# Attention's queries and keys with features on partitions, rotated there

## The chip, the cores and the metric

One core of a Trainium2 chip runs the whole program. The metric is the device time of one execution in microseconds, as the median of the timed runs. A profiled execution gives the trace from which the rows below are taken.

## What is computed

Two layers over 256 tokens of 1024 columns, in fp32: feed-forward, four mixers side by side, feed-forward. The mixers share one projection of the normed rows. The fourth is attention: 12 heads of 128 features (three groups of four, with different windows), whose queries and keys have their first 32 features rotated by an angle that grows with the position.

```python
def _partial_rope(x, positions):            # x: batch, tokens, heads, 128
    half = ROPE_DIM // 2                    # ROPE_DIM = 32
    inv_freq = ROPE_THETA ** (-jnp.arange(half) / half)
    ang = positions[..., None] * inv_freq
    cos, sin = jnp.cos(ang)[:, :, None, :], jnp.sin(ang)[:, :, None, :]
    x1, x2 = x[..., :half], x[..., half:ROPE_DIM]
    rot = jnp.concatenate([x1 * cos - x2 * sin, x2 * cos + x1 * sin], axis=-1)
    return jnp.concatenate([rot, x[..., ROPE_DIM:]], axis=-1)

def _dilated_attention(qkv, positions):
    ...
    q = _partial_rope(qkv[:, :, 0], positions)
    k = _partial_rope(qkv[:, :, 1], positions)
    v = qkv[:, :, 2]
    ...                                     # for each group: softmax(q k^T / sqrt(128), window) v
```

The other three mixers are a gated recurrence (HGRN2), a state-space model (S5) with a gated product "glu", and a convolution over 31 tokens. Each mixer's output passes a branch product, is gated and summed; then come an output product and the second feed-forward.

## The kernel before

Every product with weights is made of three matmuls in fp32r: weights and activations are each split exactly into a high and a low part, and high x high, high x low and low x high are summed in PSUM (`mm3`). `Stream` loads the weights in the order of their use (1 MB at a time on SP's queue, four buffers "raw"), and splits them slot by slot (128 x 1024): ScalarE writes the high part "whi", VectorE the low part "wlo" as a difference. Six and five buffers of these (`NW = 5`, line 29) let the splitting run ahead of TensorE.

There are two forms of product. `cols_tok` (line 803) has tokens on the output's partitions: the activations are stationary and 512 columns of weights move; two banks of 128 tokens, 24 matmuls each. It takes its slots one by one. `cols_feat` (line 849) has features on the output's partitions: weights are stationary, and all 256 tokens move; a bank holds two blocks of 128 features, 48 matmuls of 256 columns. It takes two slots at once.

Between the products run side jobs, generators for S5, the recurrence, the convolution and attention. A step of a job is issued at a `tick` inside a product, where the estimates kept by `Paced` say that its operands are there and that VectorE and ScalarE are not more than `LAG = 3.8` us (convolution: `LAST_LAG = 1.8`) behind TensorE (line 35). Each engine then works its instructions in that fixed order. Jobs have a priority: attention's rotation 0, attention 1, recurrence 2, convolution 3. `finish` issues what is left of a job where a product needs its result: S5 before "glu", the others before their branch (order of the branches: S5, recurrence, attention, convolution as number 2). Four PSUM banks "acc" take the products, four banks "mx" all side work.

`ORDER` (line 305) is the order of the mixers' products: i, u, f, q, g, then six attention chunks, the convolution's b and a, three more chunks, glu, gates and branches. An attention chunk is 512 columns by `cols_tok`: four pieces (a head's query, key or value of one group), in the order of `PIECES` (line 290): for each pair of heads all queries, then keys, then values. `ev_att` (line 1347) has ScalarE copy queries and keys from PSUM into "rq", values into "av". `rope_turn` (line 1323) rotates on VectorE ("ropeB", "ropeA", "rq": four instructions for both halves of the tokens, with tables "cosd" and "sind" by tokens), then TensorE turns each head's 128 x 128 onto feature partitions ("rt", banks of "mx"), and ScalarE copies the turned heads into "aq" and "ak". `attend` (line 1370) then multiplies queries and keys ("as"), masks, takes exponentials, turns the probabilities ("pTb") and multiplies with the values ("apv"). In the recurrence, "hd" and "hl" are small products; "y", "w", "yk" belong to S5.

Of the kernel before, what the change touches and what calls it, by code (L numbers as in the profile page):

```python
# [16 lines left out]
ALU = mybir.AluOpType  # L17
# [72 lines left out]
class ActCost:  # L90
    """With the loads of the functions' tables."""
# [22 lines left out]
class Stream:  # L114
    """Weights in the order of their use: loads, then an exact split into two 12-bit parts.

    A group is (loads, slots): loads are (source, blocks of 128 rows), slots (load, view -> part of it)."""

# [35 lines left out]
    def pump(self, n=1, ahead=True):  # L154
        """The low part of a slot whose high part is there, then the high part of the next."""
# [33 lines left out]
def trunk(ctx, tc, x_in, positions, ffn1_norm, ffn1_w_gate, ffn1_w_up, ffn1_w_down, mix_norm, w_in,  # L189
# [44 lines left out]
    def g_tok(w, pieces, n_loads=2):  # L234
        """512 columns in 2 or 4 loads; slots of 256 rows."""
# [11 lines left out]
    def g_feat(w, c0, n=512):  # L247
        """n columns; slots of 512 rows and 256 columns."""
# [8 lines left out]
    def g_rows_feat(w, order):  # L257
        """512 rows, 1024 columns; slots of all rows and 256 columns, given by the first columns of their halves."""
# [31 lines left out]
    PIECES = [(k, 2 * hp + e, g) for hp in range(2) for k in range(3) for g in range(3) for e in range(2)]  # L290

    def att_runs(i):
        return [(C_ATT + 1536 * k + 512 * g + P * h, 2 * P) for k, h, g in PIECES[4 * i:4 * i + 4:2]]

    def by_head(pieces):
        """Pairs of heads' pieces: (pair, which of it, head, kind, first group, number of pairs)."""
        a = 0
        while a < len(pieces):
            k, h, g = pieces[a]
            n = 2 if a + 2 < len(pieces) and pieces[a + 2][0] == k else 1  # L300
            for e in range(2):
                yield a // 2, e, h + e, k, g, n
            a += 2 * n

    ORDER = [("i",), ("u",), ("f",), ("q",), ("g",)] + [("att", i) for i in range(6)] + [("b",), ("a",)] + \
        [("att", i) for i in range(6, 9)] + \
# [57 lines left out]
    def grab(n=1):  # L364
        """Banks of the side work's own, held over several steps."""
# [50 lines left out]
    # rows of 128 features, turned into columns of scalars  # L416
# [28 lines left out]
    cosd = const([P, 2, 32], "cosd")  # L445
    sind = const([P, 2, 32], "sind")
# [15 lines left out]
    def masks():  # L462
        # the attention's masks: d = t - s
# [14 lines left out]
    def prepare():  # L478
        # the recurrence's masks: s in the left block whose right neighbour has t
# [10 lines left out]
        # columns  # L490
# [22 lines left out]
        # rotary tables  # L513
# [8 lines left out]
        # cos(a) = sin(pi/2 - |reduced a|)  # L522
# [4 lines left out]
        yield  # L527
        S.activation(sind[:, :, 16:32], red, AF.Sin)
# [19 lines left out]
        # S5: the discretized states of both layers, 128 states a column  # L548
# [24 lines left out]
        # mag - 1, by tanh where it is small  # L573
# [31 lines left out]
    # S5 of a layer: blocks of 4 tokens, t = 4 n + i; groups of 16 channels G = 16 jp + 2 jh + g,  # L605
    # states on partitions (g, p) and columns j = 8 jp + jh, a block's inputs on partitions (jp, i, c)
# [5 lines left out]
    def s5_tables(l):  # L612
# [15 lines left out]
        # powers of the states' factors  # L628
# [23 lines left out]
        # the discretized inputs' matrices  # L652
# [979 lines left out]
```

## Time and profile before

| | us |
|---|---|
| timed runs: median (lowest to highest of 3) | 1610.09 (1608.42 to 1613.12) |
| profiled execution, first to last instruction (span) | 1609.4 |
| TensorE busy (matmuls) | 1583.1 |
| VectorE busy | 1109.6 |
| ScalarE busy | 837.6 |
| GpSimd busy | 23.9 |

The busy time of an engine is a sum over the span; a matmul's recorded duration reaches beyond the start of the next one, because matmuls overlap, so that the distance between two starts is what a matmul takes of TensorE's time. Line 72 is the helper through which every instruction of the four engines is issued, so the rows are told apart by the names of the tiles. Layer 0's mixers run from some 210 to 617 us, layer 1's from some 1005 to 1411 us.

### The profile page before, as it was taken

What the parts mean: (1) busy time and instruction counts of PE and PEld (TensorE: products, weight loads), DVE (VectorE), ACT (ScalarE), POOL (GpSimd) and SP (SyncE); (2) the same over time, 40 slices, a digit from 0 to 9 for tenths busy, and PEclk for the clock granted to TensorE, in tenths of its full rate; (3) what the DMA queues carried; (4) which work ended last, traced back from release to release, by engine and by line L of the source; (5) the groups of instructions that cost most, each with busy time, mean ns of one, the idle gap of its engine ahead of it and who ended that gap; (6) DMA issues with size and microseconds to landing.
All of it is one profiled execution on the core that took longest, in us unless ns stands there. A gap on an engine that the chain in (4) does not pass through costs nothing.

```text
span 1609.4 us, 27748 instructions
## 1 busy us (share of the span) xinstructions
PE 1583.1 (98%) x11471; PEld 1442.8 (90%) x11471; DVE 1109.6 (69%) x1806; ACT 837.6 (52%) x1195; POOL 23.9 (1%) x53
## 2 busy tenths in 40 slices
PE   7999999999999999999999999999999999999998
PEld 6999788789899997999889988987899999989986
DVE  6778865876778866555478774567867898665553
ACT  5445455557565465444345544646565555654442
POOL 1000000000000000000000000000000000000000
PEclk9999999999999999999999999999999999999999
DMA  8565556444444456555555545664444545645551
GB/s 278 185 177 210 171 186 191 154 141 148 147 168 158 159 186 219 184 175 207 181 173 187 184 161 193 206 194 119 170 131 148 190 161 168 212 158 184 185 212 61
DMA packets 179519, 282.48 MB, mean 176 GB/s; under 512 B 26718, under 2 KB 82080, under 8 KB 179392
## 3 DMA queue, kind: packets, MB, share of 16 engines
q1 hardware_dynamic: 154240, 270.55, 49.7%
q10 hardware_dynamic: 24832, 9.97, 2.7%
q8 instruction: 90, 1.47, 0.4%
q14 instruction: 37, 0.30, 0.1%
q0 software_dynamic: 320, 0.18, 0.0%
HBM read 277.53 MB, written 3.15 MB: 174 GB/s over the span
## 4 chain that ended last, share of the span: by engine, by line
PE 94%; ACT 2%; DVE 2%; ACTq 1%; issue 1%; DMA 0%; SPq 0%; POOLq 0%; POOL 0%; DVEq 0%
PE down L72 15%; PE att_t L72 12%; PE up_h L72 12%; PE gate_h L72 12%; PE pgt_h L72 11%; PE br L72 6%; PE gate_t L72 3%; PE po_t L72 3%; PE up_t L72 2%; PE hl L72 2%; PE pi_t L72 1%; PE pa_h L72 1%; PE pb_h L72 1%; PE pg_t L72 1%; PE pq_h L72 1%; PE pf_h L72 1%
## 5 line engine op out<-in xcount | busy, mean ns | idle before, releaser
L72 DVE TENSOR_TENSOR wlo<-raw,whi 128x1024 fp32r<-128x1024 f32 x512 | 614.7, 1220 | 185.7 <-ACT whi L72 85.4
L72 ACT ACTIVATE whi<-raw 128x1024 fp32r<-128x1024 f32 x512 | 525.5, 1053 | 175.9 <-PE down L72 102.7
L72 PE MATMUL gate_h<-hTh,wlo 128*128 128x256 f32 x576 | 161.0, 280 | 2.8 <-DVE wlo L72 2.8
L72 PE MATMUL up_h<-hTh,wlo 128*128 128x256 f32 x576 | 160.9, 279 | 0.8 <-DVE wlo L72 0.8
L72 PE MATMUL gate_h<-hTh,whi 128*128 128x256 f32 x576 | 161.6, 280 | 0.0
L72 PE MATMUL up_h<-hTh,whi 128*128 128x256 f32 x576 | 161.1, 280 | 0.0
L72 PE MATMUL gate_h<-hTl,whi 128*128 128x256 f32 x576 | 160.4, 278 | 0.0
L72 PE MATMUL up_h<-hTl,whi 128*128 128x256 f32 x576 | 160.3, 278 | 0.0
L72 PE MATMUL pgt_h<-hTh,whi 128*128 128x256 f32 x512 | 145.6, 284 | 0.0
L72 PE MATMUL pgt_h<-hTh,wlo 128*128 128x256 f32 x512 | 142.6, 278 | 0.0
L72 PE MATMUL pgt_h<-hTl,whi 128*128 128x256 f32 x512 | 142.5, 278 | 0.0
L72 PE MATMUL down<-whi,gh 128*128 128x512 f32 x352 | 140.0, 398 | 0.0
L72 PE MATMUL down<-wlo,gh 128*128 128x512 f32 x352 | 139.2, 395 | 0.0
L72 PE MATMUL down<-whi,gl 128*128 128x512 f32 x352 | 139.1, 395 | 0.0
L72 PE MATMUL att_t<-whi,hTh 128*128 128x512 f32 x288 | 118.2, 410 | 0.0
L72 PE MATMUL att_t<-wlo,hTh 128*128 128x512 f32 x288 | 113.8, 395 | 0.0
L72 PE MATMUL att_t<-whi,hTl 128*128 128x512 f32 x288 | 113.8, 395 | 0.0
L72 PEld LDWEIGHTS gate_h<-hTh,wlo 128*128 128x128 f32 x576 | 108.1, 188 | 3.2 <-DVE wlo L72 3.2
L72 PEld LDWEIGHTS up_h<-hTh,wlo 128*128 128x128 f32 x576 | 108.1, 188 | 1.0 <-DVE wlo L72 1.0
L72 PEld LDWEIGHTS gate_h<-hTl,whi 128*128 128x128 f32 x576 | 108.3, 188 | 0.0
L72 PEld LDWEIGHTS up_h<-hTl,whi 128*128 128x128 f32 x576 | 108.3, 188 | 0.0
L72 PEld LDWEIGHTS up_h<-hTh,whi 128*128 128x128 f32 x576 | 107.8, 187 | 0.2
(375 smaller groups left out, 3357.7 us busy)
## 6 DMA issues: line engine op xcount, KB each, us to landing
raw<-in_w_in_dram SPq DMA_DIRECT2D x60, 1024.0 KB, 5.1
raw<-in_ffn_w_up_dram SPq DMA_DIRECT2D x44, 1024.0 KB, 5.2
raw<-in_ffn_w_down_dram SPq DMA_DIRECT2D x44, 1024.0 KB, 4.9
raw<-in_ffn_w_gate_dram SPq DMA_DIRECT2D x42, 1024.0 KB, 5.1
raw<-in_w_in_dram SPq DMA_DIRECT2D x72, 512.0 KB, 4.5
raw<-in_w_branch_dram SPq DMA_DIRECT2D x16, 1024.0 KB, 5.0
raw<-in_w_out_dram SPq DMA_DIRECT2D x8, 1024.0 KB, 5.0
raw<-in_s_w_glu_dram SPq DMA_DIRECT2D x16, 256.0 KB, 3.8
```

What stands on the lines that cost most here:

```text
L72: return f(*args, **kw)
```

## The change

Queries and keys are projected by `cols_feat`, 256 columns (the same piece of two heads) at a time, so that they come out with features on partitions and need no turning. Values keep tokens on partitions: two groups by `cols_tok`, the third by a new half-width form. The rotation works on the 32 first partitions: VectorE shuffles the 32 rows of the bank by 16 partitions ("other"), GpSimd multiplies this with the sine (its sign in the table), VectorE multiplies the copied rows with the cosine and adds the two. The tables are turned once, by four transposes in `prepare`. The order of the products becomes: six groups of queries and keys and the values of the first two heads, b and a, then those of the other two heads. `attend` waits until its heads' rotations are done. The rest of the diff takes comments away.

```diff
-    ORDER = [("i",), ("u",), ("f",), ("q",), ("g",)] + [("att", i) for i in range(6)] + [("b",), ("a",)] + \
-        [("att", i) for i in range(6, 9)] + \
+    ATT = [[("qk", hp, k, g) for k in range(2) for g in range(3)] + [("v", hp), ("v2", hp)] for hp in range(2)]
+    def c_att(k, g, hp):
+        return C_ATT + 1536 * k + 512 * g + 2 * P * hp
+    ORDER = [("i",), ("u",), ("f",), ("q",), ("g",)] + ATT[0] + [("b",), ("a",)] + ATT[1] + \
...
-            elif what == "att":
-                g_tok(w_in[l], att_runs(arg[0]))
+            elif what == "qk":
+                hp, k, g = arg
+                g_feat(w_in[l], c_att(k, g, hp), 256)
+            elif what == "v":
+                g_tok(w_in[l], [(c_att(2, g, arg[0]), 2 * P) for g in range(2)])
+            elif what == "v2":
+                g_feat(w_in[l], c_att(2, 2, arg[0]), 256)
...
+        yield
+        b = mx_bank("preprope")
+        for k, d in enumerate((cosd, sind)):
+            for t in range(2):
+                c0 = 256 * k + P * t
+                T.transpose(b[:32, c0:c0 + P], d[:, t, :], ident)
+        V.tensor_copy(rope.rearrange("r k t -> r (k t)"), b[:32, :])
...
+    def cols_tok_half(hT, evac, name):
+        slots = [ws.take() for _ in range(2)]
+        bank = acc_bank(name)
+        for t in range(2):
+            tc_ = slice(t * P, (t + 1) * P)
+            for kk in range(8):
+                if kk == 4:
+                    tick(pump=False)
+                hi, lo = slots[kk // 4]
+                mm3(bank[:, t * 256:(t + 1) * 256], hT[0][kk // 4][:, kk % 4, tc_], hT[1][kk // 4][:, kk % 4, tc_],
+                    hi[:, kk % 4, :], lo[:, kk % 4, :], kk == 0, kk == 7)
+            if t == 0:
+                tick()
+        ws.done(2)
+        evac(bank)
+        tick()
...
-        def rope_turn(raw, pieces, name):
...
-            V.tensor_tensor(B[:, :, :, 0:16], rv[:, :, :, 16:32], s1, op=ALU.mult)
-            V.tensor_tensor(B[:, :, :, 16:32], rv[:, :, :, 0:16], s2, op=ALU.mult)
-            V.tensor_tensor(A, xa, cb, op=ALU.mult)
-            V.tensor_tensor(xa, A, B, op=ALU.add)
-            yield
-            for t in range(2):
-                b = tr_bank(f"{name}{t}")
-                for i in range(n):
-                    T.transpose(b[:, i * P:(i + 1) * P], rv[:, t, i, :], ident)
-                bv = b[:, :n * P].rearrange("p (a e q) -> p a e q", e=2, q=P)
-                for a, e, h, k, g, m_ in by_head(pieces):
-                    S.activation(att[k, h][:, g:g + m_, t * P:(t + 1) * P], bv[:, a:a + m_, e, :], AF.Copy)
-            yield
+        def ev_qk(hp, k, g):
+            def ev(half, bank):
...
+                S.activation(dst, bank.rearrange("p (e q) -> p e q", e=2), AF.Copy)
+                other = H2([32, 2, 256], "other")
+                V.stream_shuffle(other.rearrange("p e q -> p (e q)"), bank[0:32, :],
+                                 [(i + 16) % 32 for i in range(32)])
+                cos, sin = (rope[:, i, None, :].to_broadcast([32, 2, 256]) for i in range(2))
+                turning[hp] += 1
+                def turn():
+                    yield
+                    G.tensor_tensor(other, other, sin, op=ALU.mult)
+                    V.tensor_tensor(dst[0:32], dst[0:32], cos, op=ALU.mult)
+                    yield
+                    V.tensor_tensor(dst[0:32], dst[0:32], other, op=ALU.add)
+                    turning[hp] -= 1
+                start(turn())
+            return ev
...
         def attend(h):
-            q, k, v = (att[i, h] for i in range(3))
+            while turning[h // 2]:
+                yield
+            q, k = ([qk(i, h, g) for g in range(3)] for i in range(2))
+            v = att["v", h]
...
-                        T.matmul(b[:, g * P:(g + 1) * P], q[:, g, qs], k[:, g, 0:P], start=True, stop=True)
+                        T.matmul(b[:, g * P:(g + 1) * P], q[g][:, qs], k[g][:, 0:P], start=True, stop=True)
...
-            elif what == "att":
-                ci = arg[0]
-                cols_tok(hT, ev_att(ci), f"att{ci}")
-                for h in range(4):
-                    if (18 * (h // 2) + 17) // 4 == ci:
-                        gens[3] = start(attend_all(h, gens.get(3)), 1)
+            elif what == "qk":
+                cols_feat(hT, ev_qk(*arg), "qk%d%d%d" % tuple(arg), 256)
+            elif what == "v":
+                cols_tok(hT, ev_v(arg[0]), f"att{arg[0]}")
+            elif what == "v2":
+                cols_tok_half(hT, ev_v2(arg[0]), f"atv{arg[0]}")
+                for h in (2 * arg[0], 2 * arg[0] + 1):
+                    gens[3] = start(attend_all(h, gens.get(3)), 1)
```

## Rows read from the trace of the kernel before

**Rows 1.** The page's head: busy us (share of span) of each engine; the chain.

```profile
PE 1583.1 (98%) x11471; PEld 1442.8 (90%) x11471; DVE 1109.6 (69%) x1806; ACT 837.6 (52%) x1195; POOL 23.9 (1%) x53
...
PE 94%; ACT 2%; DVE 2%; ACTq 1%; issue 1%; DMA 0%; SPq 0%; POOLq 0%; POOL 0%; DVEq 0%
```

**Rows 2.** The chain of waits in order of time: start us, us, what.

```profile
225.70 11.31 PE pu_h L72 x96
...
575.80 9.53 PE pgt_h L72 x84
585.33 10.88 PE br L72 x96
...
1085.93 16.81 PE att_t L72 x72
```

**Rows 3.** Groups of TensorE's instructions: busy us, mean ns | idle before.

```profile
L72 PE MATMUL att_t<-whi,hTh 128*128 128x512 f32 x288 | 118.2, 410 | 0.0
...
L72 PE MATMUL rt<-ident,rq 128*128 128x128 f32 x96 | 13.4, 276 | 1.7 <-DVE att L72 1.7
```

**Rows 4.** Timeline around three "rt" blocks of layer 0: start us, us, what [idle before].

```profile
290.85 1.04 PE L72 MATMUL rt<-ident,rq 128*128 128x128 f32 x8
...
291.64 0.48 PE L72 MATMUL att_t<-whi,hTh 128*128 128x512 f32 x1
...
291.96 0.39 PE L72 MATMUL att_t<-wlo,hTh 128*128 128x512 f32 x1
...
312.50 1.09 PE L72 MATMUL rt<-ident,rq 128*128 128x128 f32 x8
...
314.77 1.16 PE L72 MATMUL hd<-qT,kT 128*128 128x128 f32 x8 [1.18 <-ACT ak L72]
...
318.36 0.66 PE L72 MATMUL rt<-ident,rq 128*128 128x128 f32 x4
...
321.07 1.16 PE L72 MATMUL hd<-qT,kT 128*128 128x128 f32 x8 [0.53 <-DVE yk L72]
```

**Rows 5.** Timeline of VectorE: first instruction of a rotation, first one after it.

```profile
309.80 0.48 DVE L72 TENSOR_TENSOR ropeB<-rq,sind 128x128 f32<-128x128 f32 x2
...
311.00 1.22 DVE L72 TENSOR_TENSOR wlo<-raw,whi 128x1024 fp32r<-128x1024 f32 x1
```

**Rows 6.** Timeline of VectorE: from PSUM (uc, us), then from SBUF.

```profile
276.58 0.68 DVE L72 TENSOR_TENSOR uc<-w,ctab 128x512 f32<-128x512 f32 x1
277.19 0.68 DVE L72 TENSOR_TENSOR us<-w,stab 128x512 f32<-128x512 f32 x1
...
338.76 0.69 DVE L72 TENSOR_TENSOR lf<-lf 128x512 f32<-128x512 f32 x1
339.36 1.22 DVE L72 TENSOR_TENSOR wlo<-raw,whi 128x1024 fp32r<-128x1024 f32 x1
340.50 1.31 DVE L72 COPY_PREDICATED att<-hmask,hl 128x512 f32<-128x512 uint8 x1
```

**Rows 7.** GpSimd: an iota by its group, then timelines of "bmv" and VectorE.

```profile
L72 POOL IOTA dd<- 128x256 int32 x1 | 0.3, 341 | 0.0
...
551.68 0.56 POOL L72 TENSOR_TENSOR bmv<-bmv,neghalf 128x1 f32<-128x1 f32 x1 [131.59 <-DVE bmv L72]
567.66 1.49 POOL L72 TENSOR_TENSOR bmv<-bmv,neghalf 128x1 f32<-128x1 f32 x1 [15.43 <-DVE bmv L72]
...
567.51 1.23 DVE L72 TENSOR_TENSOR wlo<-raw,whi 128x1024 fp32r<-128x1024 f32 x1
```

**Rows 8.** Timeline of VectorE: the last instruction of layer 0's convolution.

```profile
579.27 0.69 DVE L72 TENSOR_TENSOR yCl<-yc,yCh 128x512 fp32r<-128x512 f32 x1 [4.03 <-ACT yCh L72]
```

**Rows 9.** Stretches of layer 0: length, busy us of PE, PEld, DVE, ACT, POOL.

```profile
273.00:307.00 34.00, 34.00 (x269) 27.33 (x268) 31.79 (x39) 16.97 (x22) 0.13 (x1) 1.00 0.46 150
...
273.00:585.00 312.00, 309.43 (x2428) 286.62 (x2427) 245.10 (x414) 185.25 (x287) 4.53 (x5) 1.00 0.48 157
```

More of the change, by code (lines that the diff above doesn't have):

```diff
@@ L289, in trunk @@
     BR_ORDER = [(2 * i, 2 * i + 1) for i in range(4)]
[L290 to L303, printed above, removed]
-    ORDER = [("i",), ("u",), ("f",), ("q",), ("g",)] + [("att", i) for i in range(6)] + [("b",), ("a",)] + \
-        [("att", i) for i in range(6, 9)] + \
+    ATT = [[("qk", hp, k, g) for k in range(2) for g in range(3)] + [("v", hp), ("v2", hp)] for hp in range(2)]
+    def c_att(k, g, hp):
+        return C_ATT + 1536 * k + 512 * g + 2 * P * hp
+    ORDER = [("i",), ("u",), ("f",), ("q",), ("g",)] + ATT[0] + [("b",), ("a",)] + ATT[1] + \
         [("glu",), ("gate", 1), ("branch", 1), ("gate", 0), ("branch", 0), ("gate", 3), ("branch", 3),
@@ L444, in trunk @@
     omlbs = const([P, 4], "omlbs")
-    cosd = const([P, 2, 32], "cosd")
-    sind = const([P, 2, 32], "sind")
+    rope = const([32, 2, 256], "rope")
     amask = const([P, 3, 256], "amask")
@@ L527, in prepare @@
         yield
+        cosd, sind = H2([P, 2, 32], "cosd"), H2([P, 2, 32], "sind")
         S.activation(sind[:, :, 16:32], red, AF.Sin)
@@ L1321, in mixers @@
         yd = [None, None]
-        def rope_turn(raw, pieces, name):
-            n = len(pieces)
-            rv = raw[:, :, :n * P].rearrange("p t (h d) -> p t h d", d=P)
-            xa = rv[:, :, :, 0:32]
-            A = tiny([P, 2, 4, 32], "ropeA", 1)[:, :, :n]
-            B = tiny([P, 2, 4, 32], "ropeB", 1)[:, :, :n]
-            cb = cosd[:, :, None, :].to_broadcast([P, 2, n, 32])
-            s1 = sind[:, :, None, 0:16].to_broadcast([P, 2, n, 16])
-            s2 = sind[:, :, None, 16:32].to_broadcast([P, 2, n, 16])
-            V.tensor_tensor(B[:, :, :, 0:16], rv[:, :, :, 16:32], s1, op=ALU.mult)
-            V.tensor_tensor(B[:, :, :, 16:32], rv[:, :, :, 0:16], s2, op=ALU.mult)
-            V.tensor_tensor(A, xa, cb, op=ALU.mult)
-            V.tensor_tensor(xa, A, B, op=ALU.add)
-            yield
-            for t in range(2):
-                b = tr_bank(f"{name}{t}")
-                for i in range(n):
-                    T.transpose(b[:, i * P:(i + 1) * P], rv[:, t, i, :], ident)
-                bv = b[:, :n * P].rearrange("p (a e q) -> p a e q", e=2, q=P)
-                for a, e, h, k, g, m_ in by_head(pieces):
-                    S.activation(att[k, h][:, g:g + m_, t * P:(t + 1) * P], bv[:, a:a + m_, e, :], AF.Copy)
-            yield
@@ L1347, in ev_att @@
-        def ev_att(ci):
-            pieces = PIECES[4 * ci:4 * ci + 4]
-            raw = {}
-            def ev(t, bank):
-                for k, h, g in pieces:
-                    if (k, h) not in att:
-                        att[k, h] = H([P, 2, 384] if k == 2 else [P, 3, 256], f"a{'qkv'[k]}{h}")
-                qk = [i for i, p_ in enumerate(pieces) if p_[0] < 2]
-                if qk:
-                    n = len(qk)
-                    if t == 0:
-                        raw[0] = H([P, 2, 512], f"rq{ci}")
-                    S.activation(raw[0][:, t, :n * P], bank[:, qk[0] * P:(qk[0] + n) * P], AF.Copy)
-                    if t == 1:
-                        start(rope_turn(raw[0], [pieces[i] for i in qk], f"rt{ci}"))
-                vs = [i for i, p_ in enumerate(pieces) if p_[0] == 2]
-                bv = bank[:, vs[0] * P:(vs[-1] + 1) * P].rearrange("p (a e q) -> p a e q", e=2, q=P) if vs else None
-                for a, e, h, k, g, m_ in by_head([pieces[i] for i in vs]):
-                    S.activation(att[k, h][:, t, g * P:(g + m_) * P].rearrange("p (a q) -> p a q", q=P),
-                                 bv[:, a:a + m_, e, :], AF.Copy)
+        turning = [0, 0]
@@ new lines, in qk @@
+        def qk(k, h, g):
+            hp, e = h // 2, h % 2
+            return att["qk"[k], hp][:, g, e, :] if g < 2 else att["2", hp][:, k, e, :]
+        def ev_qk(hp, k, g):
+            def ev(half, bank):
+                if g < 2:
+                    if g == 0:
+                        att["qk"[k], hp] = H([P, 2, 2, 256], f"a{'qk'[k]}{hp}")
+                    dst = att["qk"[k], hp][:, g]
+                else:
+                    if k == 0:
+                        att["2", hp] = H([P, 2, 2, 256], f"a2{hp}")
+                    dst = att["2", hp][:, k]
+                S.activation(dst, bank.rearrange("p (e q) -> p e q", e=2), AF.Copy)
[13 more added lines that the diff above has]
+            return ev
@@ new lines, in ev_v, with ev_v2, ev @@
+        def ev_v(hp):
+            def ev(t, bank):
+                bv = bank.rearrange("p (g e q) -> p g e q", g=2, e=2)
+                for e in range(2):
+                    h = 2 * hp + e
+                    if t == 0:
+                        att["v", h] = H([P, 2, 384], f"av{h}")
+                    S.activation(att["v", h][:, t, 0:2 * P].rearrange("p (g q) -> p g q", g=2), bv[:, :, e, :], AF.Copy)
+            return ev
+        def ev_v2(hp):
+            def ev(bank):
+                bv = bank.rearrange("p (t e q) -> p t e q", t=2, e=2)
+                for e in range(2):
+                    S.activation(att["v", 2 * hp + e][:, :, 2 * P:3 * P], bv[:, :, e, :], AF.Copy)
@@ L1393, in attend @@
                     for g in range(2):
-                        T.matmul(b[:, g * 256:(g + 1) * 256], q[:, g, qs], k[:, g, :], start=True, stop=True)
+                        T.matmul(b[:, g * 256:(g + 1) * 256], q[g][:, qs], k[g], start=True, stop=True)
                     b2 = mx_bank("as2")
-                    T.matmul(b2[:, 0:256], q[:, 2, qs], k[:, 2, :], start=True, stop=True)
+                    T.matmul(b2[:, 0:256], q[2][:, qs], k[2], start=True, stop=True)
                     yield
```

## The prediction

> **What bounds the kernel now.** I read the head of the page first: TensorE is busy for 1583.1 of 1609.4 us, VectorE for 1109.6, ScalarE for 837.6, GpSimd for 23.9, and the chain of work that ended last is TensorE for 94% of the span [rows 1]. A matmul's recorded duration is no cost here, though: the mean "att_t" matmul is 410 ns long [rows 3], but they start every 233.5 ns (16.81 us for 72 of them), because they overlap. So every product below is priced from the chain of waits in order of time, whose rows are stretches with nothing in between: 233.5 ns for one of 512 columns, 117.8 ns (11.31 us for 96) for most of 256 columns, and 113.3 ns (10.88 us for 96) for some others of 256 [rows 2]. What is worth time is therefore only what adds or removes time on TensorE's own queue, or makes it wait. The timeline around the turned heads and the stretches' busy times then tell what stands on that queue and how much room VectorE has to take more.
>
> **What the change removes.** Per layer, 48 transposes "rt" (96 in the trace [rows 3]) in seven blocks.
> - Undisturbed, a block of eight holds the queue from 290.85 to 291.64, 0.79 us or 0.099 us a transpose; the next matmul then starts 0.32 us after the first one behind it, where 0.233 is the rule, so a block that stands alone costs 0.09 us more [rows 4].
> - Two blocks are not undisturbed. The one at 312.50 holds the queue until "hd" starts at 314.77, 2.27 us; the next from 318.36 to 321.07, 2.71 us [rows 4]. The row of "hd" names the cause: it waits for ScalarE's copy of a turned head ("ak"), because the four banks of "mx" are then taken by two "y" and two "rt". Without "rt" the two "y" and the two "hd" fill exactly four, so I count these waits as gone.
> - Sum of a layer: 2.27 + 2.71 + 32 others x 0.099 (3.17) + about four restarts x 0.09 (0.36) = 8.5 us; the second layer repeats the pattern. Both: 17.0 us off TensorE.
>
> **What the products cost afterwards.** Before: 9 chunks x 48 matmuls of 512 columns, 432 x 0.2335 = 100.9 us a layer. After: 12 groups of queries and keys and two halves of values have 48 matmuls of 256 columns each, 672 x 0.1178 = 79.2; two groups of values stay 48 of 512, 96 x 0.2335 = 22.4. Sum 101.6, so +0.7 us a layer, +1.4 in both. The half products of values (tokens on partitions, 256 columns moving) have no row of their form; the two prices of 256 columns bound them, and I take the commoner. If all 1344 new ones ran at 113.3, it would be 1344 x 4.5 ns = 6.0 us less.
>
> **What else it adds.** Four transposes and a copy for the rotary table, once: 4 x 0.099 + 0.09 = 0.5 us. ScalarE loses the 64 copies of turned heads and gains none, and at 837.6 us it bounds nothing [rows 1]. The DMAs carry the same weights in the same 1 KB rows, in fewer issues on SP, so they cost nothing. "attend" waits until both heads' rotations are done; between the last group of queries and keys of a half and its first "attend" stand the values' products (11.2 + 5.65 us), so that wait is covered. Convolution's projections move ahead of one and a half chunks of attention, some 17 us, which helps it.
>
> VectorE pays. It loses rotations of 1.20 us for four pieces (309.80 to 311.00 [rows 5]); seven of these a layer, two of them with half the pieces, some 7.6 us. It gains, for each of 12 groups, a shuffle, a product and a sum over 32x512. None is in the trace; the nearest rows are products of 128x512, which follow each other in 0.61 us from PSUM and 0.60 from SBUF [rows 6]. Below, a quarter of the partitions could cost less, but these rows grow with the columns alone (1024 columns: 1.14 [rows 6]), so I take 0.605 x 3 = 1.81 us a group, 21.8 a layer, +14.2 net. The Trainium skill, "VectorE: DVE Perf Modes", section on the rules for kernel authors, gives some 2400 ns for a shuffle of [32, 2048], by which 512 columns would be an estimated 0.6 us; the sum would be the same.
>
> GpSimd gets one product of 32x512 a group. Its rows: 0.56 us for a product of one column and 0.34 for an iota of 256 columns [rows 7]. Below: twice the iota, 0.68; above: 0.56 + 2 x 0.68 = 1.9, if reading costs as much as writing; I take 0.56 + 0.68 = 1.24. It is 12 x 1.24 = 15 us a layer on an idle engine; what counts is whether VectorE must stand still meanwhile. The same GpSimd operation "bmv" takes 0.56 us at 551.68, with VectorE idle, and 1.49 us at 567.66, where VectorE subtracts "wlo" from 567.51 for 1.23 us [rows 7]: GpSimd ended 0.4 us after that subtraction. So one waits for the other, in this direction at least. The Trainium skill, "SBUF — State Buffer", section "Who interferes with whom", states the rule: a VectorE instruction with two SBUF inputs and a GpSimd one that reads SBUF exclude each other, and whichever comes first keeps the port for its whole length. By that rule VectorE would stand still too, for GpSimd's whole product, and nearly everything in its queue has two SBUF inputs; no row here shows that direction.
>
> **Has VectorE the room?** From the first attention product to branch 2 (273 to 585) it works 245.1 of 312 us [rows 9]. Afterwards: 245.1 + 14.2 = 259.3 of some 304.5, and 274 if it stands still for all of GpSimd's 15: full cover, 30 to 45 us. Convolution, the last to be needed, ends at 579.96 [rows 8], before branch 2 at 585.33 [rows 2]. It is tight locally: from 273 to 307 VectorE works 31.8 of 34.0 us [rows 9], and that is where the first six groups land. A group of 5.65 us has two splits of weights (2 x 1.14) and 1.81 of rotation, which leaves 1.56 us for S5 and for standing still. S5 is pushed back (it has until "glu", some 80 us later). The planner (LAG) lets VectorE run 3.8 us behind TensorE; three split slots lie ahead at a group's start, 3 x 2.83 = 8.5 us; so 4.7 us are to spare. The planner's costs know nothing of standing still: six groups x 1.24 = 7.4 us, at worst 2.7 us too much. In the second half only convolution fills (1.8 us), 6.7 to spare, at worst 0.7. Worst: (2.7 + 0.7) x 2 layers = 6.8 us of waits for "wlo"; least: 0. I take 2.0, as the lock is partly met by times when VectorE waits anyway.
>
> **The sum.** -17.0 + 1.4 + 0.5 + 2.0 = -13.1 us. The profiled span is 1609.4, the median of the timed runs 1610.1 (1608.4 to 1613.1), so 0.7 lies around it: 1610.1 - 13.1 = 1597.0 us.
>
> **The rivals.**
> - The waits of 2.27 and 2.71 don't go. They were 1.48 and 1.92 more than the transposes, 6.8 us in both layers. For: they stand where S5, the recurrence and ScalarE's table loads meet, and the order there shifts. Against: the banks suffice. 1597.0 + 6.8 = 1603.8.
> - VectorE stands still for each product, uncovered: 6.8 instead of 2.0, and as much again if the sum waits for GpSimd in its queue (the product itself first waits for up to 1.2 us of VectorE's work): 1602 to 1609, centre 1605. By the skill's port rule above this is the case to expect at its milder end.
> - Slower: the rotation becomes the bound. Standing still and waiting beyond 1.56 us a group means that VectorE can't split weights as fast as TensorE takes them, even with all side work stopped. GpSimd's product at its upper price of 1.9 plus a wait of 0.7 for it is 2.6, 1.0 too much, x 24 groups = 25 us: 1597.0 - 2.0 + 25 = 1620 (up to 1635 as convolution comes late too). For: 31.8 of 34.0. Against: three values groups between the halves give time to catch up.
> - The faster price of 256 columns: 1597.0 - 6.0 = 1591. For: both prices occur in the same kernel, for the same product ("pgt_h" takes 9.53 us for 84 at 575.80, 113.5 ns [rows 2]). Against: the projections before attention are all at 117.8.
>
> **How the numbers follow.** Forecast 0.47; waits stay 0.12; standing still 0.16; slower 0.15; faster price 0.10. A difference within 0.3% (4.8 us) can't be told from no change here. Faster by more (below 1605.3): 0.47 + 0.12 + 0.10 and a bit over a quarter of the third = 0.73; within: the rest of the third and the edge of the fourth, 0.13; slower: 0.14. The range 1589 to 1609 holds the forecast, the waits, nearly all of the third and most of the last, 0.81; it leaves out the slower case.
>
> **What would show it.** After: no "rt" block; 12 runs of 48 matmuls of 256 columns a layer at 0.118; "hd" right behind "y" without a wait on ScalarE; TensorE's waits for "wlo" in attention between 0 and 7 us in all; VectorE some 14 us busier per layer from the first attention product to branch 2. Wrong if the groups' stretches are longer than 5.65 us with "wlo" as releaser (then the slower case), if GpSimd's product is over 2 us, or if TensorE waits at branch 2 for convolution.

## The result: slower by 0.8%

After the change the median is 1623.6 us (1620.3 to 1624.6), beside 1610.7 for the kernel before in the same sitting: 1.0081 times as long (interval 1.0061 to 1.0100). The prediction was 1597.0, with 1589 to 1609 as its range: wrong in the direction. The page of the profiled execution after, its head and its chain (busy us, share of the span, instructions of each engine):

```profile
span 1622.4 us, 28851 instructions
...
PE 1583.6 (98%) x12051; PEld 1474.7 (91%) x12051; DVE 1160.5 (72%) x1847; ACT 816.7 (50%) x1115; POOL 101.2 (6%) x77
...
PE 88%; DVE 6%; ACT 2%; issue 2%; DMA 1%; ACTq 0%; SPq 0%; POOL 0%; POOLq 0%; DVEq 0%
```

Against [rows 1], VectorE has 50.9 us more, GpSimd 77.3, and the chain has become 6% VectorE where it was 2%: TensorE now waits for VectorE. Where it happens follows from the starts of the same products in both traces (us by which each stretch became longer; negative: shorter):

| stretch | layer 0 | layer 1 |
|---|---|---|
| up to attention's first product | +3.0 | -1.3 |
| attention's products, with convolution's b and a, up to "glu" | -0.2 | -0.4 |
| glu, gates and branches, up to branch 2 (convolution) | -0.8 | -0.8 |
| branch 2 itself | +7.4 | +7.1 |
| from there to the end | | -1.1 |

Two rows tell it: attention's stretch, where the transposes went, gained next to nothing, and branch 2 lost 7 us in each layer. The waits of TensorE after (us in total, times, the longest):

```profile
PE xT L72 <- DVE xn L72: 9.3, 1, 9.3
PE br L72 <- ACT yCh L72: 8.4, 2, 4.2
PE y L72 <- DVE W L72: 5.4, 2, 2.7
PE hl L72 <- DVE ER L72: 4.5, 2, 3.0
```

The first is the program's beginning and was there before (8.8 us). "br", "y" and "hl" are new: convolution, S5 and the recurrence. No product of queries and keys waits for a "wlo". The stretches after (length, busy us of PE, PEld, DVE, ACT and POOL, granted clock, DMA share, GB/s):

```profile
273.00:585.00 312.00, 306.15 (x2753) 298.93 (x2750) 268.60 (x432) 171.45 (x244) 43.19 (x17) 0.99 0.50 160
331.00:337.00 6.00, 2.98 (x27) 2.81 (x25) 6.00 (x10) 1.29 (x2) 0.00 (x0) 1.00 0.06 21
337.00:344.00 7.00, 7.00 (x48) 7.00 (x48) 1.20 (x3) 3.08 (x4) 0.00 (x0) 0.76 0.47 75
587.00:606.00 19.00, 14.65 (x104) 14.06 (x102) 9.40 (x13) 8.39 (x11) 0.00 (x0) 0.82 0.17 56
```

Against [rows 9], VectorE is busy for 268.6 instead of 245.1 of the 312 us, and TensorE for 3.3 us less. From 331 to 337 VectorE is full and TensorE half empty. And behind the waits for "hl" and at branch 2 the granted clock is low: 0.76 from 337 to 344, 0.82 from 587 to 606. Behind the wait for "y" it stays at 1.00 (from 325.69 to 332.60).

How the wait for "hl" comes about, in the timeline of VectorE (start us, us, what) and of TensorE:

```profile
328.44 0.67 DVE L72 TENSOR_TENSOR ak<-ak,rope 32x512 f32<-32x512 f32 x1
329.04 0.67 DVE L72 TENSOR_TENSOR a<-a,other 32x512 f32<-32x512 f32 x1
...
333.19 0.67 DVE L72 TENSOR_TENSOR ak<-ak,other 32x512 f32<-32x512 f32 x1
333.79 0.67 DVE L72 TENSOR_TENSOR a<-a,other 32x512 f32<-32x512 f32 x1
334.39 0.67 DVE L72 TENSOR_TENSOR att<-hd,ident 128x512 f32<-128x512 f32 x1
334.99 0.67 DVE L72 TENSOR_TENSOR ER<-ER,qT 128x512 f32<-128x512 f32 x1
...
335.81 1.97 PE L72 MATMUL hl<-ER,KL 128*128 128x64 f32 x16 [3.02 <-DVE ER L72]
337.59 0.47 PE L72 MATMUL atv<-whi,hTh 128*128 128x256 f32 x1
337.85 0.42 PE L72 MATMUL atv<-wlo,hTh 128*128 128x256 f32 x1
338.06 0.41 PE L72 MATMUL atv<-whi,hTl 128*128 128x256 f32 x1
```

From 328.4 to 334.4 VectorE works seven instructions of rotations that had piled up; "ER", which "hl" needs, stands behind them. TensorE's order is fixed, so the 36 products "atv" behind "hl" wait too, although nothing is missing for them. Afterwards these products start every 0.213 us (337.85, 338.06) instead of 0.118: the lower of TensorE's two levels (1.2 of 2.4 GHz). The 36 take 5.85 us where 36 x 0.1178 = 4.24 was the price.

The wait for "y" comes a little earlier:

```profile
322.22 2.29 DVE L72 TENSOR_TENSOR wlo<-raw,whi 128x1024 fp32r<-128x1024 f32 x1
324.43 1.21 DVE L72 TENSOR_TENSOR W<-W,W 128x1024 f32<-128x1024 f32 x1
...
325.69 0.34 PE L72 MATMUL y<-W,C 64*64 64x63 f32 x8 [2.67 <-DVE W L72]
```

The "wlo" ahead of "W" takes 2.29 us instead of 1.22, beside a product of GpSimd that runs from 320.13 to 323.42. In the kernel before, "W" was ready at 308.74 and "y" came at 311.57.

### The profile page after: what moved, and what is told of

The parts are those of the page before. It is cut to its first block, busy times and chain, and to the rows that moved or that the text cites. A ratio compares the mean times of both kernels' runs of the same rounds, so it can differ in the third digit from the quotient of the medians.

```text
span 1622.4 us, 28851 instructions
## 1 busy us (share of the span) xinstructions
PE 1583.6 (98%) x12051; PEld 1474.7 (91%) x12051; DVE 1160.5 (72%) x1847; ACT 816.7 (50%) x1115; POOL 101.2 (6%) x77
## 4 chain that ended last, share of the span: by engine, by line
PE 88%; DVE 6%; ACT 2%; issue 2%; DMA 1%; ACTq 0%; SPq 0%; POOL 0%; POOLq 0%; DVEq 0%
PE down L72 15%; PE up_h L72 12%; PE gate_h L72 12%; PE pgt_h L72 10%; PE qk_h L72 6%; PE br L72 6%; PE po_t L72 3%; PE gate_t L72 3%; DVE wlo L72 2%; PE up_t L72 2%; PE hl L72 2%; PE pi_t L72 1%; PE pg_t L72 1%; PE pa_h L72 1%; PE pb_h L72 1%
## 5 line engine op out<-in xcount | busy, mean ns | idle before, releaser
L72 PE MATMUL qk_h<-hTh,whi 128*128 128x256 f32 x384 | 109.6, 286 | 0.0
L72 PEld LDWEIGHTS gate_h<-hTh,whi 128*128 128x128 f32 x576 | 108.7, 189 | 0.1
L72 PE MATMUL qk_h<-hTh,wlo 128*128 128x256 f32 x384 | 107.6, 280 | 0.3
```

The lines of the kernel that those rows point to most:

```text
L72: return f(*args, **kw)
```

## The experiments

The open question was which part of the addition costs the time: VectorE's own three instructions a group, GpSimd's product (by holding VectorE up, or by coming late), or the products on TensorE themselves. Ratios are to the kernel before.

**1. No rotation at all.** What remains is the change on TensorE.

```diff
-                other = H2([32, 2, 256], "other")
-                V.stream_shuffle(...)
...
-                    G.tensor_tensor(other, other, sin, op=ALU.mult)
-                    V.tensor_tensor(dst[0:32], dst[0:32], cos, op=ALU.mult)
...
-                    V.tensor_tensor(dst[0:32], dst[0:32], other, op=ALU.add)
```

> Left out: the whole rotation (shuffle, both products, sum); queries and keys are copied unrotated. What TensorE itself gains and pays stays. Theories P and V: the prediction's terms for TensorE alone (-17.0 + 1.4 + 0.5, and some 2 to 3 us lost in the first feed-forward), so 1596 to 1600, and no wait of more than 1 us at y, hl, branch 2. Rival L: the waits at y, hl and branch 2 stay, 1610 to 1623.

Measured: 1594.9 us, 0.9902 (0.9888 to 0.9917). Attention's stretch is 7.9 us shorter than before in both layers, and no wait above 1.9 us is left but the first. VectorE, which rotates nothing here, is busy for 240.6 us of the stretch from 273 to 585. So the products and the lost transposes bring what they were priced at, and the whole loss, 28.7 us against the changed kernel, is the rotation's.

**2. No product on GpSimd.** VectorE's three instructions stay.

```diff
-                    G.tensor_tensor(other, other, sin, op=ALU.mult)
```

> Left out: GpSimd's product of the shuffled rows with the sine (24 in all); shuffle, cosine product and sum stay, so the rotation isn't whole. Theory P (VectorE is held up by GpSimd's products, 1.1 us each time they meet: 12 x 1.1 = 13 us a layer, and that makes the results late): the waits of y, hl and branch 2 go, about 14.5 us a layer back, 1594 to 1602 us. Rival V (VectorE's own three instructions a group are the load, 12 x 1.9 = 23 us a layer against 7.6 before): 1615 to 1624, branch 2 still waits some 3 us or more. Rival L (the waits come from the new order of the products, whatever VectorE does): unchanged, 1623.

Measured: 1612.1 us, 1.0005 (0.9995 to 1.0015), between the first two expectations. The same stretch, and TensorE's longest waits but the first:

```profile
273.00:585.00 312.00, 306.80 (x2727) 299.93 (x2725) 259.42 (x433) 177.15 (x251) 5.46 (x5) 0.99 0.50 161
```

```profile
PE br L72 <- ACT yCh L72: 8.4, 2, 4.2
PE hl L72 <- DVE ER L72: 3.1, 2, 1.6
```

VectorE's own three instructions thus eat the whole gain: 17.2 us against experiment 1. GpSimd's product costs 11.5 us more, and with it VectorE's busy time falls from 268.6 to 259.4. "y" doesn't wait any more and "hl" 1.6 us instead of 3.0; convolution is as late without the product.

**3. The product on VectorE, nothing on GpSimd.**

```diff
-                    G.tensor_tensor(other, other, sin, op=ALU.mult)
+                    V.tensor_tensor(other, other, sin, op=ALU.mult)
                     V.tensor_tensor(dst[0:32], dst[0:32], cos, op=ALU.mult)
-                    yield
                     V.tensor_tensor(dst[0:32], dst[0:32], other, op=ALU.add)
```

> The sine product runs on VectorE, in one step with the cosine product and the sum; nothing is left out. VectorE gains 0.6 us a group of its own work and loses the meetings with GpSimd (1.1) and the wait for it. Theory P: 12 x 0.5 = 6 us a layer less for VectorE, and the planner now counts all of it: 1602 to 1613. Rival V: VectorE has 12 x 0.6 = 7 us more work a layer, later still: 1625 to 1640. Rival L: 1623.

Measured: 1625.7 us, 1.0093 (1.0078 to 1.0109). VectorE is busy for 263.7 us of the stretch. The waits change their names ("hl" 4.9, "cB" 4.9, the branches 6.1: 15.9 us, beside 18.3 for "br", "y" and "hl" in the changed kernel) more than their sum: moving the product back from GpSimd is no way out.

**4. The kernel before with VectorE's addition alone.** Three sums of 32x512 that nobody reads, after each of eight chunks.

```diff
                 cols_tok(hT, ev_att(ci), f"att{ci}")
+                if ci < 8:
+                    def extra():
+                        yield
+                        for _ in range(3):
+                            V.tensor_tensor(scr, amask[0:32, 0:2, :], amask[0:32, 0:2, :], op=ALU.add)
+                    scr = H2([32, 2, 256], "scr")
+                    start(extra())
```

> The kernel before, with 24 additions of 32x512 a layer on VectorE, three behind each of eight attention chunks, whose result nobody uses: 24 x 0.605 = 14.5 us a layer, the net load that the prediction gave the change. Theory V: no more room than in the changed kernel: waits at y, hl or branch 2, 1616 to 1628. Rival (the 67 us that VectorE idles from 273 to 585 cover it; the changed kernel's loss is in its order of work): 1610 to 1614.

Measured: 1620.8 us (1613.8 to 1625.2, the slowest of the four being the profiled one), 1.0073 (1.0044 to 1.0103). VectorE's busy time in the stretch goes from [rows 9]'s 245.1 to 256.8, less than was predicted for the change (259.3). Two of the waits that appear:

```profile
PE hl L72 <- DVE ER L72: 4.7, 2, 3.4
PE hl L72 <- DVE KL L72: 3.2, 2, 1.6
```

Load on VectorE is thus enough, with no GpSimd product, no new products on TensorE and no result that anybody waits for: some 30 us of work (both layers; 1140.0 us busy in the whole span instead of 1109.6) on an engine that is idle for 21% of the stretch cost 11.4 us. It is not the same loss in every part: branch 2 doesn't wait here and takes its 10.88 us.

**5. GpSimd's product unread.** It has as much to do, on other operands, but waits for no shuffle, and the sum doesn't wait for it.

```diff
-                    G.tensor_tensor(other, other, sin, op=ALU.mult)
+                    G.tensor_tensor(H2([32, 2, 256], "free"), amask[0:32, 0:2, :], sin, op=ALU.mult)
```

> The changed kernel, where GpSimd's product of the same size works on other data into a tile that nobody reads: VectorE is still held up by it, but no longer waits for its result (left out: the sine in the rotation). Theory P (being held up costs the 11.5 us that the kernel without product gained): 1618 to 1626. Rival (the chain shuffle, product, sum costs it, and the side work that waits for it): 1609 to 1615.

Measured: 1616.2 us, 1.0035 (1.0020 to 1.0049), between the two expectations. VectorE is busy for 267.8 us of the stretch, nearly as in the changed kernel. Against experiment 2, 4.2 us come from the product's work; the other 7.3 up to the changed kernel would be what it costs that the sum waits for it. But the order of the side work shifts between these kernels as well, and the product itself is shorter here (2.35 us in the mean instead of 3.14), so the split is rough.

**6. GpSimd's product twice.**

```diff
                     G.tensor_tensor(other, other, sin, op=ALU.mult)
+                    G.tensor_tensor(other, other, sin, op=ALU.mult)
```

> The changed kernel with GpSimd's product done twice (the sine enters squared). Without the product the time fell by 11.5 us. If GpSimd holds the port for its whole product, VectorE stands still up to another 13 us a layer: 1630 to 1645. Rival (what the product costs is its chain, shuffle to product to sum): the sum comes 1.2 to 2.2 us later, 1623 to 1627.

Measured: 1621.4 us, 1.0081 (1.0062 to 1.0101): not slower than the changed kernel. VectorE's busy time rises to 274.1, products do now wait for "wlo" (7.0 us in all), but branch 2 doesn't wait and takes its 10.88 us. So the loss isn't proportional to GpSimd's time: a different step comes late, according to where the ticks put the side work.

**7. The convolution earlier.** The changed kernel; convolution may put VectorE 3.2 instead of 1.8 us behind.

```diff
-LAG, TABLE_LAG, LAST_LAG = 3.8, 2.0, 1.8
+LAG, TABLE_LAG, LAST_LAG = 3.8, 2.0, 3.2
```

> The changed kernel, with the planner allowed to put VectorE 3.2 instead of 1.8 us behind TensorE for the convolution. Theory C (VectorE has no room left, so what convolution gains others lose): 1619 to 1628. Rival S (the planner starts convolution's steps too late, though VectorE has room): the wait at branch 2, 7.4 us a layer with the slower clock behind it, goes: 1606 to 1612.

Measured: 1636.1 us, 1.0169 (1.0152 to 1.0186). Branch 2 no longer waits for "yCh", but attention's own product does:

```profile
PE apv L72 <- ACT pT L72: 12.3, 4, 4.1
```

Convolution's earlier work is paid for by the others, and by more than either expectation allowed. It isn't VectorE's room that is missing at this wait: from 556.96 to 561.36 VectorE is idle. "pT" starts at 557.85 on ScalarE, behind convolution's "yc" and "yCh" (553.42 to 555.10) and two reloaded tables.

**8. The table alone.** The kernel before with the four transposes of the rotary table and their copy.

```diff
+        b = mx_bank("preprope")
+        rope = H2([32, 2, 256], "rope")
+        for k, d in enumerate((cosd, sind)):
+            for t in range(2):
+                c0 = 256 * k + P * t
+                T.transpose(b[:32, c0:c0 + P], d[:, t, :], ident)
+        V.tensor_copy(rope.rearrange("r k t -> r (k t)"), b[:32, :])
```

> The kernel before, with nothing but the table's four transposes and its copy added (its result isn't used). In the changed kernel the first feed-forward ends 2.3 us later, with matmuls of 256 columns at 117.8 instead of 113.3 ns behind these transposes. Theory: the transposes alone do that, +1.5 to +3 us (1612 to 1614), and the rows from 56 to 94 us are at 117.8. Rival: the loss comes from something else of the change, 1610.5 to 1611, with 113.3 there.

Measured: 1612.6 us, 1.0005 (0.9996 to 1.0015), no difference that can be measured. The chain of this kernel shows what four transposes can do, though (start us, us, what):

```profile
51.32 4.08 PE up_h L72 x36
55.40 0.44 PE preprope L72 x4
55.84 7.07 PE up_h L72 x60
62.91 11.31 PE gate_h L72 x96
```

36 products before them at 0.113 us, 96 after them at 0.118; in the kernel before the same block runs at 0.113 (10.88 us). It is 1 us by the end of this feed-forward, and is part of the 3.0 us that the changed kernel loses before attention. Another 1.5 us there are 70 products "gate_h" that take 10.05 us instead of 8.52, at a granted clock of 0.57 from 112 to 116; the kernel of experiment 11, which has nothing of the change, shows 10.04 for them, so they aren't the change's.

That the transposes set the distance isn't shown. In experiment 12, with the same four, 36 products before them take 4.24 us (0.118) and 96 after them 10.88 (0.113); in experiment 10 both sides are at 0.118.

**9. Three groups at once, on three quadrants.** ScalarE copies the 32 rows of each group to their own 32 partitions; shuffle, both products and sum are done once for three groups on 96 partitions, all on VectorE; ScalarE copies the rows back. The table has three copies.

```diff
+                if g == 0:
+                    rows_[k] = H2([96, 2, 256], f"rows{k}"), []
+                R, dsts = rows_[k]
+                S.activation(R[32 * g:32 * g + 32], bank[0:32].rearrange("p (e q) -> p e q", e=2), AF.Copy)
+                dsts.append(dst)
+                if g < 2:
+                    return
...
-                    G.tensor_tensor(other, other, sin, op=ALU.mult)
-                    V.tensor_tensor(dst[0:32], dst[0:32], cos, op=ALU.mult)
+                    other = H2([96, 2, 256], "other")
+                    V.stream_shuffle(other.rearrange("p e q -> p (e q)"), R.rearrange("p e q -> p (e q)"),
+                                     [(i + 16) % 32 for i in range(32)])
+                    V.tensor_tensor(R, R, cos, op=ALU.mult)
+                    V.tensor_tensor(other, other, sin, op=ALU.mult)
+                    V.tensor_tensor(R, R, other, op=ALU.add)
                     yield
-                    V.tensor_tensor(dst[0:32], dst[0:32], other, op=ALU.add)
+                    for n, d in enumerate(dsts):
+                        S.activation(d[0:32], R[32 * n:32 * n + 32], AF.Copy)
```

> Complete: ScalarE also copies the 32 rows of three groups to partitions 0, 32 and 64 of one tile; shuffle, products and sum run there once for three groups, on VectorE alone, and ScalarE copies the rotated rows back. VectorE: 4 sets x 4 x 0.605 = 9.7 us a layer instead of 21.8 and the meetings with GpSimd; ScalarE 14 us a layer more. Theory V (VectorE's load is the cause): near the kernel without rotation, 1594 to 1602, no wait at branch 2. Rival (results are late because the rotation is a chain across engines, or ScalarE is now late): 1606 to 1622.

Measured: 1615.6 us, 1.0043 (1.0028 to 1.0058): better than the changed kernel (1.0081), still slower than before, and within the rival's range. VectorE's work has shrunk as meant. Its instructions by tile (duration in ns: least, median, greatest; first and last start; shape):

```profile
L72 DVE STREAM_SHUFFLE other<-rows x8: 728/734/749, 311.7 to 1216.8; 96x512 f32<-96x512 f32 x8
L72 DVE TENSOR_TENSOR other<-other,rope x8: 678/680/682, 313.1 to 1218.2; 96x512 f32<-96x512 f32 x8
```

Its busy time in the stretch is 245.2 us, as before the change. One long wait is left, and the timeline shows that it isn't VectorE's:

```profile
325.88 5.64 ACTq L1282 DMA_DIRECT2D zd<-yk  x8
331.57 1.06 ACT L72 ACTIVATE whi<-raw 128x1024 fp32r<-128x1024 f32 x1 [5.72 <-DMA raw<-in_w_in_dram]
...
335.23 3.65 PE L72 MATMUL hl<-ER,KL 128*128 128x64 f32 x16 [7.40 <-DVE ER L72]
```

ScalarE issues S5's eight writes "zd" itself, for 5.64 us; a split's high part "whi", then VectorE's "wlo", then "ER" and "hl" stand behind it. In the kernel before, the same eight took 3.86 us, from 323.63, and no product waited behind them. The row names a DMA as releaser, but "whi" starts 0.05 us after the eight issues end (331.52); in experiment 10, which takes them off this queue, the same "whi" follows the copy of "yk" at 326.06 without a wait.

**10. The same, with these eight writes issued by GpSimd.**

```diff
-                    nc.scalar.dma_start(zv[jp, i].rearrange("c a h n -> c (a h) n"), yk[r:r + 16])
+                    nc.gpsimd.dma_start(zv[jp, i].rearrange("c a h n -> c (a h) n"), yk[r:r + 16])
```

> Complete: the kernel with three groups rotated at once, and the eight writes of S5's result (zd) issued from GpSimd instead of ScalarE. In that kernel TensorE waited 7.4 us a layer at hl and ran slower behind it, while ScalarE issued these eight writes for 5.6 us ahead of a split of weights that VectorE and then hl waited for. Theory Q (the chain hl - VectorE - ScalarE's issuing is what is left): 1594 to 1601. Rival (the result is late in any case, ScalarE's issuing only stands there): 1609 to 1616.

Measured: 1599.9 us (1599.2 to 1601.2), 0.9932 (0.9914 to 0.9951): faster than both kernels. The stretch, and the only wait of a side job that is left:

```profile
273.00:585.00 312.00, 310.46 (x2767) 303.53 (x2764) 249.90 (x408) 193.66 (x278) 9.06 (x13) 1.00 0.50 163
```

```profile
PE hl L72 <- DVE ER L72: 3.1, 2, 1.5
```

**11 and 12. The writes moved in the two kernels themselves.** The edit of experiment 10 in the kernel before, and in the changed one.

```diff
-                    nc.scalar.dma_start(zv[jp, i].rearrange("c a h n -> c (a h) n"), yk[r:r + 16])
+                    nc.gpsimd.dma_start(zv[jp, i].rearrange("c a h n -> c (a h) n"), yk[r:r + 16])
```

> Complete: the kernel before with the same eight writes issued from GpSimd. There ScalarE issues them for 3.9 us a layer at 323.6, and TensorE doesn't wait behind it. Theory Q: no change, 1607 to 1612. Rival (ScalarE's issuing costs every version the same): 1600 or less, so that the other kernel's gain isn't the rotation's.

> Complete: the changed kernel with S5's eight writes issued from GpSimd. In the changed kernel ScalarE issues them at 338, behind the waits of y and hl, and the wait at branch 2 has nothing to do with them. Theory V (VectorE's load): 1619 to 1626. Rival (ScalarE's issuing, as in the kernel with three groups at once, is the larger part of the loss): 1600 to 1612.

Measured: before with it 1611.4 us, 1.0002 (0.9992 to 1.0011); after with it 1624.4 us, 1.0085 (1.0070 to 1.0100). The move is worth nothing in either, so experiment 10's gain over both needs the rotation on three quadrants; the move alone only takes away the wait that this had called up.

## Why the prediction was wrong, point by point

**The transposes and the products (-17.0, +1.4, +0.5): right.** Experiment 1, which has these three terms and no rotation, is 16.6 us below the kernel before where they add up to 15.1, and attention's stretch in it is 7.9 us shorter in each layer where 8.5 - 0.7 = 7.8 was the sum. The waits of "hd" for "ak" went, as the banks allowed; that rival is out. (For the second block [rows 4] name VectorE's "yk" and not "ak"; that wait went too.) The faster price of 256 columns didn't come: in the changed kernel 72 products of queries and keys take 8.54 us (0.119 each), 36 others 4.24 (0.118).

**VectorE's price: right; GpSimd's: too low.** VectorE's own load came to 259.4 us (experiment 2), predicted 259.3; in the whole span it rose by 30.2 us, predicted 2 x 14.2. A shuffle on 32 partitions starts 0.64 us before what follows it (0.73 us of recorded time), a product 0.60; 0.605 was the price of each. The 0.6 us estimated for the shuffle from the Trainium skill ("VectorE: DVE Perf Modes", rules for kernel authors) agrees. The instructions by tile:

```profile
L72 DVE STREAM_SHUFFLE other<-qk_h x24: 722/730/742, 283.6 to 1221.0; 32x512 f32<-32x512 f32 x24
L72 POOL TENSOR_TENSOR other<-other,rope x24: 2087/2222/8257, 284.5 to 1221.9; 32x512 f32<-32x512 f32 x24
```

GpSimd's product was priced at 1.24 us, and "over 2" named as a sign of being wrong: it takes 2.22 in the median and up to 8.26. The timelines show that each of the two engines holds up the other:

```profile
289.93 1.19 DVE L72 TENSOR_TENSOR wlo<-raw,whi 128x1024 fp32r<-128x1024 f32 x1
291.06 1.77 DVE L72 TENSOR_TENSOR aq<-aq,other 32x512 f32<-32x512 f32 x1
...
301.97 4.45 DVE L72 TENSOR_TENSOR_SCAN W<-rt,W 128x1024 f32<-128x1024 f32 x2
...
290.11 2.18 POOL L72 TENSOR_TENSOR other<-other,rope 32x512 f32<-32x512 f32 x1 [3.47 <-DVE other L72]
299.28 10.49 POOL L72 TENSOR_TENSOR other<-other,rope 32x512 f32<-32x512 f32 x2 [7.00 <-DVE other L72]
```

GpSimd's product that starts at 290.11 ends at 292.29, 1.2 us after "wlo" did (291.12), so its own work is near the price and the rest is waiting; VectorE's sum at 291.06 takes 1.77 us instead of 0.67, the 1.1 us more that GpSimd then works. The longest product, the first of the two in the last row, runs for 8.26 us from 299.28 to 307.54, beside two "wlo", a sum and two scans (4.45 us together); the "wlo" behind these takes 1.62 us instead of 1.22, and "X", beside the next product, 2.30 instead of 1.21. So the direction that no row of before showed does exist: 268.6 - 259.4 = 9.2 us a layer, 0.77 for each of 12 products (by the whole spans 1160.5 - 1139.8 = 20.7 us, 0.86 for each of 24). The Trainium skill ("SBUF — State Buffer", section "Who interferes with whom") has the rule that the port goes whole to whoever comes first. Both directions agree with it, the order not always: behind the product of 299.28, VectorE's sum of 300.23, "wlo" of 300.83 and scans of 301.97 came later and were still worked first, the first two in their usual 0.67 and 1.21 us.

**"Full cover" is the step that failed.** The prediction added up VectorE's idle time from the first attention product to branch 2, found 30 to 45 us of it, and then asked only whether the weights' low parts would come in time. They did: no product waits for "wlo" in attention, and the 2.0 us set down for that were too much. What came late are the results of side work. That S5 may be "pushed back" as "it has until "glu", some 80 us later" is wrong in itself: S5's "y" is a product on TensorE with its place in the queue (322.68), and whatever stands behind it waits until "W" is there. The same holds for "hl". And there was less room than [rows 8] show: before, the distance from the result to its use was 5.4 us for convolution, but 2.8 for "y" and 3.1 for "hl".

```profile
307.53 1.21 DVE L72 TENSOR_TENSOR W<-W,W 128x1024 f32<-128x1024 f32 x1
319.74 0.68 DVE L72 TENSOR_TENSOR ER<-ER,qT 128x512 f32<-128x512 f32 x1
...
311.57 0.30 PE L72 MATMUL y<-W,C 64*64 64x63 f32 x8
323.47 1.90 PE L72 MATMUL hl<-ER,KL 128*128 128x64 f32 x16
```

In layer 0's attention after the change, the waits of 2.7 and 3.0 us and the 1.6 us of low clock behind "hl" are 7.3 us; the stretch should have become 7.8 us shorter and became 0.2 shorter.

**Convolution: the warning sign was in the document, and was taken for room.** [Rows 8] have its end at 579.96, 5.4 us before branch 2. The prediction let it be "full cover" and said that its projections come 17 us earlier. In the changed kernel (timelines of ScalarE and TensorE at branch 2):

```profile
580.96 0.60 ACT L72 ACTIVATE gate<-pgt_h 128x512 f32<-128x512 f32 x1 [4.04 <-PE pgt_h L72]
...
589.31 1.28 ACT L72 ACT_TABLE_LOAD   x1
590.61 1.02 ACT L72 ACTIVATE yc<-cB,vcol 128x256 f32<-128x256 f32 x2
591.66 0.63 ACT L72 ACTIVATE yCh<-yc 128x512 fp32r<-128x512 f32 x1
...
592.34 0.58 PE L72 MATMUL br<-yCh,whi 128*128 128x256 f32 x1 [4.21 <-ACT yCh L72]
...
594.09 0.41 PE L72 MATMUL br<-yCh,wlo 128*128 128x256 f32 x1
594.30 0.41 PE L72 MATMUL br<-yCh,whi 128*128 128x256 f32 x1
```

Its last steps fall to ticks behind the last gate products, and on ScalarE's queue behind gates that wait for TensorE (4.04 us) and behind reloaded tables; "yCl" ends at 593.0 instead of 580.0. ScalarE had such waits and reloads before, too (a gate there waits 5.15 us, at 567.90); what is new is the place: the last "cB" starts at 586.85, 0.35 us before branch 2, where it was 575.21, 10.0 us before it. The branch waits 4.2 us and then runs at the lower clock level (0.213 us a product), and takes 18.3 us instead of 10.9. The delay goes by steps: without GpSimd's product (experiment 2) VectorE has 9 us less to do, and "yCl" still ends 5.8 us after the branch's start in both (586.2 and 580.4; 593.0 and 587.2). That fits a step which, once it misses its tick, goes to the next, a product later. That the rotation's load brings the wait about is shown in so far as it is gone in experiments 1, 9 and 10, which have less of that load; why it is convolution that comes late isn't: with still more load (experiment 6), and with load put on the kernel before (experiment 4), convolution was in time and others were late.

**The rivals.** The slower rival's time, 1620, came out, and its cause only in part. VectorE did become the bound in stretches (6.00 of 6.00 us from 331 to 337), but not because weights couldn't be split. The rival of VectorE standing still (1605) had the right mechanism, some 0.8 us a product where up to 1.24 was allowed, and a price taken from the same wrong place, waits for "wlo".

**What no term had: the clock.** All waits were priced at their own length. Behind a wait of 3 to 4 us came 1.6 us (at "hl") and 3.2 us (at branch 2: 18.3 - 10.9 - 4.2) of products at the lower level. Of the 14.5 us that branch 2 lost in both layers, some 6 are this. The length of the wait doesn't settle it: in experiment 2 products start every 0.213 us behind a wait of 1.6 us for "hl", and in the changed kernel none do behind the 2.7 us for "y".

**What stays open.** No rate leads from VectorE's load to time: the busy times in the stretch and the medians were 240.6 and 1594.9 (experiment 1), 249.9 and 1599.9 (10), 259.4 and 1612.1 (2), 263.7 and 1625.7 (3), 268.6 and 1623.6 (the change), 274.1 and 1621.4 (6). From the first to the third of these, 18.8 us of VectorE a layer cost 17.2 us of time; above, more load isn't more time. Experiments 4 (256.8 and 1620.8), 5 (267.8 and 1616.2) and 9 (245.2 and 1615.6, with the load of before) lie off that line. The stretch is cut at fixed times, so in a later kernel a little work falls behind its end. How much of the 11.5 us of GpSimd's product is port and how much is the sum's wait was settled only roughly (experiment 5).

## What to carry to other kernels

Work that is put on an engine's idle time is covered only if each result on that engine has room until its own use: in a kernel whose TensorE takes side products in a fixed order, look for the smallest such distances (2.8, 3.1 and 5.4 us here), not for the sum of idle time, and allow for the lower clock in the price of a wait. A rotation on feature partitions uses 32 of 128 partitions and pays for the columns: stacking the rows of three groups on three quadrants put four instructions in the place of twelve and, with eight DMA issues moved, turned a loss of 0.8% into a gain of 0.7%. When a relieved engine leaves one long wait behind, look at what its neighbour's queue issues: eight DMA issues on ScalarE, without a wait behind them before, held up a whole chain.

## What the runs showed of the chip that was not expected

- On VectorE the number of partitions made no difference, also for the shuffle: 0.73 us for 32x512 and for 96x512, and 0.67 to 0.68 for a product of 32x512, 96x512 and 128x512.
- A GpSimd product with both inputs in SBUF lengthened VectorE's instruction by up to 1.1 us and was itself held up by VectorE's, at worst to 8.26 us in all where 2.22 is the median.
- Eight DMA issues held ScalarE's queue for 3.86 us in the kernel before and for 5.64 in experiment 9, 0.5 to 0.7 us each.
- Products of 256 columns start every 0.113 or every 0.118 us at the full clock, for a whole block of a feed-forward, and the same products differ in this from one kernel to the next (51 to 75 us, experiments 8, 10 and 12). What decides it is open.
